# The modulation weights' tiles are loaded one step ahead of their multiplies, and the multiplies get a fixed place on VectorE

## The chip, the cores and the metric

The kernel runs on one core of a Trainium2 chip. The metric is the device time of one execution in microseconds (us); lower is better. Engines are named as in the profile: PE is TensorE's matmuls and PEld its weight loads, DVE is VectorE, ACT is ScalarE, POOL is GpSimd, and SP is SyncE, which here only issues DMA transfers (SPq is its queue).

## What is computed

Two transformer-like blocks run one after the other on 256 tokens of width 2048, in fp32. The part that matters here is the first block, whose normalised inputs, residuals and FFN are scaled by six vectors that come from a conditioning vector `c`:

```
silu_c = jax.nn.silu(c)                                    # [1, 2048]
mod_l = jnp.split(silu_c @ w_mod[l] + b_mod[l], 6, axis=-1) # w_mod: [2048, 6*2048]
hl  = modulate(rms_norm(xl, norm1_g[l]), mod_l[0], mod_l[1])
xl  = xl + mod_l[2][:, None, :] * mixer_output(...)
hl2 = modulate(rms_norm(xl, norm2_g[l]), mod_l[3], mod_l[4])
xl  = xl + mod_l[5][:, None, :] * sq_relu_ffn(hl2, w_ff1[l], b_ff1[l], w_ff2[l], b_ff2[l])
```

`mod_l[0]` and `mod_l[1]` are needed at once. The other four vectors, 64 tiles of 128 outputs, are needed only later: `mod_l[2]` to `mod_l[4]` in the output projection, `mod_l[5]` in the FFN.

## The kernel before

Every large matrix product goes through the same chunk of work. `weights` loads one chunk of a weight matrix, [128, 2048] fp32, as two halves of [128, 1024] (512 KB each) into the pool `raw`, which has four buffers, so two chunks. `split_w` makes two tiles out of each half: `wh`, a rounded copy that ScalarE writes (L198), and `wl`, what the rounding left out, which VectorE makes by a subtraction (L199). Both have three buffers. PE then multiplies by `wh` and by `wl`: in `gemm` (L213, L214) 16 pairs of matmuls per chunk with 512 and 256 columns, in `gemm_w` (L204 to L206) three of 258 columns. A `raw` buffer is free for its next load when its `wl` is done, so the load of a half waits for the subtraction of the half that stands four places ahead of it.

The 64 late tiles of the modulation don't go to PE. `w_mod` is stored with outputs on partitions, and for each tile VectorE multiplies two halves of [128, 1024] by a row `bc` that holds silu(c) on every partition, and sums along the row (`mod_tile`, a SCALAR_TENSOR_TENSOR with an accumulated output, L80 in the profile, since all VectorE calls go through a helper). Their tiles are called `mraw` and lie in the pool `aux`, which has two buffers. `qkv` puts 64 such steps into a list `fill`, and `weights` takes one of them out after every second chunk, 128 chunks in all: the query projection, the three branches of the mixer with their gates, the output projection and the first quarter of the FFN's first layer. In the trace that is the stretch from 353 us to 1233 us. A chunk with 512 + 256 columns and two of them between fillers are the unit below: "a step" is two chunks, four halves, one `w_mod` tile.

Nobody writes the order of the instructions by hand. A scheduler lays them out on each engine by priorities and dependencies; work inside `low()` has a low priority and goes where the scheduler finds room. `late` ties an instruction behind the last matmul that has been written so far, as an order for the scheduler alone, without a semaphore. Each engine then runs its instructions in that order, and SP issues all loads of `raw` and `mraw` in one queue.

Of the kernel before, what the change touches and what calls it, by code (L numbers as in the profile page):

```python
# [10 lines left out]
F32 = mybir.dt.float32  # L11
# [3 lines left out]
ALU = mybir.AluOpType  # L15
# [74 lines left out]
class Net:  # L90
# [65 lines left out]
            return self.vecs[:, o:o + c]  # L156
        return self.vecs[:, o + i:o + i + n]

    def late(self, inst):

        i = getattr(inst, "ins", inst)
        d = mybir.DependencyInfo(mybir.DependencyClass.NoSync, mybir.DependencyReason.SCHED_ONLY)
        self.tc.add_manual_dep(i, self.last_mm.name, d, reason="late")
        return inst

    def after(self, inst):

        i = getattr(inst, "ins", inst)
        d = mybir.DependencyInfo(mybir.DependencyClass.Sync, mybir.DependencyReason.DATA)
        self.tc.add_manual_dep(i, self.last_mm.name, d, reason="after")  # L170
        return inst
# [23 lines left out]
    def split_w(self, raw, n):  # L195
        h = self.wp.tile([P, 1024], F32R, name="wh", tag="wh", bufs=3)
        l = self.wp.tile([P, 1024], F32R, name="wl", tag="wl", bufs=3)
        self.nc.scalar.activation(h[:, :n], raw, AF.Copy)  # L198
        self.nc.vector.tensor_sub(l[:, :n], raw, h[:, :n].bitcast(F32))  # L199
        return h, l  # L200

    def mm3(self, ps, lh, ll, rh, rl, start, stop):
# [136 lines left out]
                                                            ap=[[0, P], [1, 2048]])))  # L339
        self.a.activation(self.bc, self.bc, AF.Silu)  # L340

    def mod_tile(self, i):

        for hf in range(2):
            s = slice(hf * 1024, hf * 1024 + 1024)
            raw = self.aux("mraw")
            self.late(self.nc.sync.dma_start(raw, self.ins["w_mod"][i][:, s]))
            self.v.scalar_tensor_tensor(raw, raw, 1.0, self.bc[:, s], op0=ALU.mult, op1=ALU.mult,
                                        accum_out=self.modt[:, i, hf:hf + 1])

    def startup(self):

# [137 lines left out]
    def qkv(self):  # L490
        v, a, ins = self.v, self.a, self.ins
        for m in range(2):
            pss = self.gemm(ins["w_k"][m], [self.hx, self.hc])
            for s, ps in enumerate(pss):
                a.activation(self.kT[1][:, 2 + m, s * T:s * T + T], ps, AF.Identity, bias=self.vec("b_in", 46 + m))
        self.vt = self.many("D2 A3", [P, 2, 1024], "vt")
        for g in range(2):
            vb = self.t2("vb")
            self.bcast_row(vb, "na_vb", g * 512)
            pss = self.gemm_tok([ins["w_v"][g, c] for c in range(4)], [self.hx, self.hc])  # L500
            s = slice(g * 512, g * 512 + 512)
            for i, ps in enumerate(pss):
                v.tensor_add(self.vt[i // 2][:, i % 2, s], ps, vb)
        self.q = self.at("C0", [P, 8, T], "q")
        self.load_bc()
        self.fill = [lambda i=i: self.mod_tile(i) for i in (*range(32, 80), *range(80, 96))]
        for m in range(8):
            ps, = self.gemm(ins["w_q"][m], [self.hx])
            v.tensor_scalar(self.q[:, m, :], ps, self.vec("b_in", 32 + m), 0.125, op0=ALU.add, op1=ALU.mult)
# [1038 lines left out]
```

## Time and profile before

| | |
|---|---|
| median of 3 runs | 2786.59 us (2778.81 to 2793.52) |
| profiled execution | 2797.3 us, span 2795.5 us |
| busy share of PE, DVE, ACT | 96%, 74%, 52% of the span |
| mean granted PE clock | 0.987 |
| largest wait of VectorE for a DMA | 168.8 us in 65 waits, for `mraw` |
| chain that ended last | PE 26%, DVE 2%, ACT 1% of the span; the rest of it is not shown there |

The three runs differ by 0.5% of their median. The profiled execution is 10.7 us above the median. A PE that counts as busy is one with a matmul under way by a modelled end, so gaps between matmuls are a lower bound of what PE loses.

### The profile page before, as it was taken

The page shows a single profiled execution, that of the slowest core. Times are in us where ns is not written, and L with a number is a line of the kernel's source. Part 1 is how long each engine was busy: PE and PEld are TensorE (multiplying, and loading weights), DVE is VectorE, ACT ScalarE, POOL GpSimd, SP SyncE. Part 2 cuts the span into 40 slices and gives each one's busy share as a digit, 9 for nine tenths or more (in the row PEclk, how much of TensorE's full clock was granted, in tenths as well). Part 3 has the DMA queues.
Part 4 walks back from the last instruction along what each step waited for, and adds up shares of the span by engine and source line. Part 5 has one row for each costly group of instructions (what it writes and reads, how often), then busy time and mean ns, then how long its engine had stood idle before and what let it go on. Part 6 is the DMA issues. An engine that isn't in the chain of part 4 may idle for free. (4 is left out here: it accounts for less than half of the span.)

```text
span 2795.5 us, 47178 instructions
## 1 busy us (share of the span) xinstructions
PE 2691.3 (96%) x18464; PEld 2340.2 (84%) x18464; DVE 2057.0 (74%) x3559; ACT 1440.0 (52%) x2242; POOL 116.1 (4%) x222
## 2 busy tenths in 40 slices
PE   7999999999998889999999999999999999999988
PEld 6888877777877777988989989988888888888876
DVE  4579886776866667766888777677656776767987
ACT  3243265566534445544544645665545554644754
POOL 0000001110000000000000000000000001110000
PEclk9999999999999999999999999999999999999999
DMA  9854377777767777777566676755455567775544
GB/s 378 318 158 132 123 240 230 247 244 264 249 245 246 242 245 252 249 240 212 183 197 211 211 218 213 224 175 164 155 181 167 173 199 232 239 232 193 161 137 146
DMA packets 161616, 595.66 MB, mean 213 GB/s; under 512 B 19441, under 2 KB 20481, under 8 KB 156657
## 3 DMA queue, kind: packets, MB, share of 16 engines
q1 hardware_dynamic: 145152, 539.03, 59.3%
q0 software_dynamic: 16096, 53.60, 5.6%
q8 instruction: 144, 2.36, 0.4%
q14 instruction: 80, 0.65, 0.1%
q10 hardware_dynamic: 144, 0.02, 0.0%
HBM read 571.60 MB, written 17.83 MB: 211 GB/s over the span
## 5 line engine op out<-in xcount | busy, mean ns | idle before, releaser
L198 ACT ACTIVATE wh<-raw 128x1024 fp32r<-128x1024 f32 x812 | 859.3, 1059 | 938.4 <-PE pg L213 513.7
L199 DVE TENSOR_TENSOR wl<-raw,wh 128x1024 fp32r<-128x1024 f32 x812 | 990.9, 1221 | 353.3 <-ACT wh L198 344.4
L213 PE MATMUL pg<-hx,wh 128*128 128x512 f32 x1312 | 477.3, 404 | 6.0 <-ACT kT L80 3.4
L214 PE MATMUL pg<-hx,wl 128*128 128x256 f32 x1312 | 376.6, 288 | 20.2 <-DVE wl L199 20.1
L213 PE MATMUL pg<-fa,wh 128*128 128x512 f32 x1024 | 358.3, 396 | 0.0
L213 PEld LDWEIGHTS pg<-hx,wh 128*128 128x128 f32 x1312 | 251.9, 193 | 65.5 <-ACT kT L80 3.6
L206 PE MATMUL pg<-fg,wl 128*128 128x258 f32 x1024 | 287.3, 281 | 7.2 <-DVE wl L199 7.2
L205 PE MATMUL pg<-fg,wh 128*128 128x258 f32 x1024 | 290.4, 284 | 0.0
L204 PE MATMUL pg<-fg,wh 128*128 128x258 f32 x1024 | 289.0, 283 | 0.0
L214 PE MATMUL pg<-fa,wl 128*128 128x256 f32 x1024 | 284.6, 279 | 1.2 <-DVE wl L199 1.2
L80 DVE SCALAR_TENSOR_TENSOR mraw<-mraw,bc 128x1024 f32<-128x1024 f32 x128 | 156.1, 1221 | 169.7 <-DMA mraw<-in_w_mod 168.8
L214 PEld LDWEIGHTS pg<-hx,wl 128*128 128x128 f32 x1312 | 253.2, 193 | 29.7 <-DVE wl L199 24.9
L213 PEld LDWEIGHTS pg<-fa,wh 128*128 128x128 f32 x1024 | 191.7, 188 | 45.3 <-issue 0.6
L213 PE MATMUL pg<-rg,wh 128*128 128x512 f32 x640 | 228.8, 399 | 0.2 <-ACT wh L198 0.2
L213 PE MATMUL pg<-ag,wh 128*128 128x512 f32 x640 | 228.2, 400 | 0.8 <-ACT wh L198 0.8
L206 PEld LDWEIGHTS pg<-fg,wl 128*128 128x128 f32 x1024 | 194.9, 191 | 8.5 <-DVE wl L199 8.4
L214 PEld LDWEIGHTS pg<-fa,wl 128*128 128x128 f32 x1024 | 192.8, 188 | 2.3 <-DVE wl L199 1.5
L205 PEld LDWEIGHTS pg<-fg,wh 128*128 128x128 f32 x1024 | 193.5, 189 | 0.1
L204 PEld LDWEIGHTS pg<-fg,wh 128*128 128x128 f32 x1024 | 192.5, 188 | 1.1 <-issue 1.0
L214 PE MATMUL pg<-rg,wl 128*128 128x256 f32 x640 | 181.3, 284 | 0.7 <-DVE wl L199 0.7
L214 PE MATMUL pg<-ag,wl 128*128 128x256 f32 x640 | 181.2, 283 | 0.0
L213 PEld LDWEIGHTS pg<-ag,wh 128*128 128x128 f32 x640 | 120.2, 188 | 29.5 <-ACT wh L198 1.1
(487 smaller groups left out, 4874.6 us busy)
## 6 DMA issues: line engine op xcount, KB each, us to landing
raw<-in_w_f SPq DMA_DIRECT2D x256, 512.0 KB, 4.6
mraw<-in_w_mod SPq DMA_DIRECT2D x128, 512.0 KB, 7.5
raw<-in_w_g SPq DMA_DIRECT2D x96, 512.0 KB, 6.2
raw<-in_w_mod SPq DMA_DIRECT2D x20, 1024.0 KB, 8.3
raw<-in_w_conv SPq DMA_DIRECT2D x32, 512.0 KB, 3.8
raw<-in_w_o SPq DMA_DIRECT2D x32, 512.0 KB, 6.2
raw<-in_w_gab SPq DMA_DIRECT2D x32, 512.0 KB, 3.8
raw<-in_w_abo SPq DMA_DIRECT2D x32, 512.0 KB, 4.4
```

The source lines that it names most:

```text
L80: r = f(*a, **kw)
L198: self.nc.scalar.activation(h[:, :n], raw, AF.Copy)
L199: self.nc.vector.tensor_sub(l[:, :n], raw, h[:, :n].bitcast(F32))
L204: mm(ps, lhsT=lh, rhs=rh, start=start, stop=False)
L205: mm(ps, lhsT=lh, rhs=rl, start=False, stop=False)
L206: i = mm(ps, lhsT=ll, rhs=rh, start=False, stop=stop)
L213: mm(ps, lhsT=lh, rhs=act.both(b), start=start, stop=False, skip_group_check=True)
L214: i = mm(ps[:, :T], lhsT=ll, rhs=act.hi(b), start=False, stop=stop, skip_group_check=True)
```

## The change

`mod_tile` is cut in two. `mod_load(i)` takes both `aux` buffers and issues the two loads of tile i. `mod_tile(i, then)` multiplies the halves that stand in the buffers, and after that calls `mod_load` for the next tile. The first load is issued ahead of the query projection. A second edit gives the multiplies a place: `split_w` remembers its last subtraction as `last_wl`, and each multiply is ordered behind it (`behind`, an order for the scheduler without a semaphore). The number of loads, multiplies and buffers stays.

```
-    def late(self, inst):
+    def behind(self, inst, other):
         i = getattr(inst, "ins", inst)
         d = mybir.DependencyInfo(mybir.DependencyClass.NoSync, mybir.DependencyReason.SCHED_ONLY)
-        self.tc.add_manual_dep(i, self.last_mm.name, d, reason="late")
+        self.tc.add_manual_dep(i, other.name, d, reason="behind")
         return inst
+    def late(self, inst):
+        return self.behind(inst, self.last_mm)
...
         self.nc.scalar.activation(h[:, :n], raw, AF.Copy)
-        self.nc.vector.tensor_sub(l[:, :n], raw, h[:, :n].bitcast(F32))
+        i = self.nc.vector.tensor_sub(l[:, :n], raw, h[:, :n].bitcast(F32))
+        self.last_wl = getattr(i, "ins", i)
...
-    def mod_tile(self, i):
-        for hf in range(2):
+    def mod_load(self, i):
+        self.mraw = [self.aux("mraw") for _ in range(2)]
+        for hf, raw in enumerate(self.mraw):
             s = slice(hf * 1024, hf * 1024 + 1024)
-            raw = self.aux("mraw")
             self.late(self.nc.sync.dma_start(raw, self.ins["w_mod"][i][:, s]))
-            self.v.scalar_tensor_tensor(raw, raw, 1.0, self.bc[:, s], op0=ALU.mult, op1=ALU.mult,
-                                        accum_out=self.modt[:, i, hf:hf + 1])
+    def mod_tile(self, i, then):
+        for hf, raw in enumerate(self.mraw):
+            s = slice(hf * 1024, hf * 1024 + 1024)
+            self.behind(self.v.scalar_tensor_tensor(raw, raw, 1.0, self.bc[:, s], op0=ALU.mult, op1=ALU.mult,
+                                                    accum_out=self.modt[:, i, hf:hf + 1]), self.last_wl)
+        if then is not None:
+            self.mod_load(then)
...
-        self.fill = [lambda i=i: self.mod_tile(i) for i in (*range(32, 80), *range(80, 96))]
+        self.mod_load(32)
+        self.fill = [lambda i=i: self.mod_tile(i, i + 1 if i < 95 else None) for i in range(32, 96)]
```

VectorE, before, near the end of the branch that `w_no` closes, the step whose wait stands at 860.30 us in the trace. The numbers are those of buffers: `wl_8232` and `wl_8238` are the halves of the newest chunk, `mraw_8241` and `mraw_8244` the tile of this step, and `raw_8297` and `raw_8303` the halves of the chunk after.

```order
L199 TENSOR_TENSOR wl_8232<-raw_8229,wh_8231 128x1024
L80 TENSOR_TENSOR pg_8141<-pg_8141,fold_8174 128x256
L199 TENSOR_TENSOR wl_8238<-raw_8235,wh_8237 128x1024
L80 SCALAR_TENSOR_TENSOR mraw_8241,modt_79<-mraw_8241,bc_3585 128x1024
L80 SCALAR_TENSOR_TENSOR mraw_8244,modt_79<-mraw_8244,bc_3585 128x1024
L199 TENSOR_TENSOR wl_8300<-raw_8297,wh_8299 128x1024
```

The same place now, on VectorE; `wl_8236` and `wl_8242` are the halves of the same chunk.

```order
L203 TENSOR_TENSOR wl_8236<-raw_8233,wh_8235 128x1024
L80 TENSOR_TENSOR pg_8145<-pg_8145,fold_8178 128x256
L203 TENSOR_TENSOR wl_8242<-raw_8239,wh_8241 128x1024
L80 SCALAR_TENSOR_TENSOR mraw_8141,modt_79<-mraw_8141,bc_3585 128x1024
L80 SCALAR_TENSOR_TENSOR mraw_8142,modt_79<-mraw_8142,bc_3585 128x1024
L203 TENSOR_TENSOR wl_8304<-raw_8301,wh_8303 128x1024
```

At this place nothing moved on VectorE: the pair stands behind the newest chunk's second half in both. Over the 64 steps, 63 pairs now stand together, 63 of them right behind a `wl`; before it was 21 pairs that stood together and 23 first multiplies right behind a `wl`, the others having short work between or ahead of them.

SP's queue of loads, before, around the loads of that tile; what a load waits for stands in brackets (DVE is a count that VectorE's instructions raise, DMAHW are counts of earlier DMAs).

```order
L185 DMA raw_8229<-in_w_no 128x1024 [waits DMAHW3_49,DMAHW1_49,DVE_49]
L185 DMA raw_8235<-in_w_no 128x1024 [waits DMAHW4_49,DMAHW2_49,DVE_49]
L185 DMA raw_8297<-in_w_g 128x1024 [waits DMAHW5_49,DVE_49]
L185 DMA raw_8303<-in_w_g 128x1024 [waits DMAHW6_49,DVE_49]
L347 DMA mraw_8241<-in_w_mod 128x1024
L347 DMA mraw_8244<-in_w_mod 128x1024
L185 DMA raw_8347<-in_w_g 128x1024 [waits DMAHW7_49,DMAHW1_49,DVE_49]
```

And the queue now, around the loads of the tile that is multiplied at the place shown.

```order
L189 DMA raw_8233<-in_w_no 128x1024 [waits DMAHW3_49,DVE_49]
L189 DMA raw_8239<-in_w_no 128x1024 [waits DMAHW4_49,DVE_49]
L352 DMA mraw_8141<-in_w_mod 128x1024 [waits DVE_49]
L352 DMA mraw_8142<-in_w_mod 128x1024 [waits DVE_49]
L189 DMA raw_8301<-in_w_g 128x1024 [waits DMAHW7_49,DMAHW5_49,DVE_49]
L189 DMA raw_8307<-in_w_g 128x1024 [waits DMAHW6_49,DMAHW0_49,DVE_49]
L189 DMA raw_8351<-in_w_g 128x1024 [waits DMAHW1_49,DVE_49]
```

Before, the loads of a step's tile stood behind those of the chunk that follows the step's newest one (8297, 8303) and waited for nothing of their own. Now they stand one chunk earlier, right behind the step's newest chunk (8233, 8239), and each waits for VectorE: for the multiply of the tile before, which holds its buffer.

## Rows read from the trace of the kernel before

**Rows 1.** The page: span, busy time, costly groups of `mraw` and `wl`

```profile
PE 2691.3 (96%) x18464; PEld 2340.2 (84%) x18464; DVE 2057.0 (74%) x3559; ACT 1440.0 (52%) x2242; POOL 116.1 (4%) x222
...
L199 DVE TENSOR_TENSOR wl<-raw,wh 128x1024 fp32r<-128x1024 f32 x812 | 990.9, 1221 | 353.3 <-ACT wh L198 344.4
...
L80 DVE SCALAR_TENSOR_TENSOR mraw<-mraw,bc 128x1024 f32<-128x1024 f32 x128 | 156.1, 1221 | 169.7 <-DMA mraw<-in_w_mod 168.8
```

**Rows 2.** Busy time by stretch: window, length, PE, PEld, DVE, ACT, POOL, clock, DMA share, GB/s

```profile
350.00:727.00 377.00, 368.34 (x1898) 291.58 (x1897) 275.75 (x489) 240.02 (x380) 35.57 (x66) 0.99 0.76 247
727.00:1120.00 393.00, 357.37 (x1941) 305.06 (x1941) 291.53 (x462) 183.05 (x292) 5.25 (x9) 0.97 0.72 244
1120.00:1233.00 113.00, 105.37 (x835) 102.44 (x833) 79.00 (x130) 61.60 (x94) 0.00 (x0) 1.00 0.74 250
1245.00:1500.00 255.00, 255.00 (x1701) 234.07 (x1700) 196.39 (x399) 120.89 (x153) 8.03 (x15) 1.00 0.63 199
1450.00:1500.00 50.00, 50.00 (x285) 43.44 (x284) 43.99 (x86) 18.76 (x18) 4.27 (x8) 1.00 0.65 209
2350.00:2400.00 50.00, 50.00 (x351) 43.93 (x350) 33.99 (x49) 25.75 (x33) 10.53 (x22) 1.00 0.83 282
```

**Rows 3.** VectorE around 860 us: start, duration, instruction, idle time and its releaser

```profile
846.49 1.23 DVE L80 SCALAR_TENSOR_TENSOR mraw<-mraw,bc 128x1024 f32<-128x1024 f32 x1 [3.24 <-DMA mraw<-in_w_mod]
...
854.31 1.22 DVE L199 TENSOR_TENSOR wl<-raw,wh 128x1024 fp32r<-128x1024 f32 x1
860.30 1.22 DVE L80 SCALAR_TENSOR_TENSOR mraw<-mraw,bc 128x1024 f32<-128x1024 f32 x1 [4.78 <-DMA mraw<-in_w_mod]
861.46 0.08 DVE L80 DVE_READ_ACCUMULATOR mraw<-mraw,bc 128x1 f32 x1
861.57 1.23 DVE L80 SCALAR_TENSOR_TENSOR mraw<-mraw,bc 128x1024 f32<-128x1024 f32 x1
862.72 0.08 DVE L80 DVE_READ_ACCUMULATOR mraw<-mraw,bc 128x1 f32 x1
862.72 1.22 DVE L199 TENSOR_TENSOR wl<-raw,wh 128x1024 fp32r<-128x1024 f32 x1
```

**Rows 4.** PE in the same stretch

```profile
850.39 0.39 PE L214 MATMUL pg<-hx,wl 128*128 128x256 f32 x1 [1.10 <-DVE wl L199]
...
863.99 0.39 PE L214 MATMUL pg<-hx,wl 128*128 128x256 f32 x1 [2.06 <-DVE wl L199]
```

**Rows 5.** SP's queue in the same stretch: first issue, length, merged issues

```profile
850.36 2.13 SPq L185 DMA_DIRECT2D raw<-in_w_g  x2
852.54 0.90 SPq L347 DMA_DIRECT2D mraw<-in_w_mod  x2
854.09 1.79 SPq L185 DMA_DIRECT2D raw<-in_w_g  x2
```

**Rows 6.** PE's waits, 727 to 1233 us: total, times, longest

```profile
PE pg L214 <- DVE wl L199: 34.6, 21, 3.4
PE pg L206 <- DVE wl L199: 7.2, 6, 1.7
PE pg L213 <- ACT wh L198: 0.8, 1, 0.8
```

**Rows 7.** PE's longest wait, 350 to 727 us

```profile
PE pg L214 <- DVE wl L199: 4.5, 4, 1.8
```

**Rows 8.** The subtraction of L199 by stretch: length, busy (count), clock, DMA share, GB/s

```profile
727.00:1233.00 506.00, 188.07 (x155) 0.97 0.73 246
1245.00:1500.00 255.00, 110.00 (x90) 1.00 0.63 199
```

**Rows 9.** Loads 727 to 1233 us: issues, KB each, median us to landing; then `mraw`'s spread

```profile
mraw<-in_w_mod SPq DMA_DIRECT2D x76, 512.0 KB, 7.6
raw<-in_w_g SPq DMA_DIRECT2D x56, 512.0 KB, 6.6
raw<-in_w_so SPq DMA_DIRECT2D x16, 512.0 KB, 8.1
...
DMA to landing us min/median/max: 5.3/7.6/11.0
```

**Rows 10.** The same, 1245 to 1500 us

```profile
raw<-in_w_f SPq DMA_DIRECT2D x90, 512.0 KB, 4.5
```

**Rows 11.** The tile `raw`, 727 to 1233 us: ScalarE's waits for a load

```profile
  DMA raw<-in_w_g: 7.6, 4
...
  DMA raw<-in_w_no: 2.3, 1
```

## Prediction

> **What bounds the kernel now.** I began with the page. PE is busy for 2691.3 of 2795.5 us [rows 1], so most of the kernel is limited by PE, and 104 us are left in which it visibly stands. The costly groups name a suspect: VectorE sat idle for 168.8 us ahead of the `mraw` multiplies until their DMA had landed [rows 1]. Idle time of VectorE counts only if PE waits for it, so I went to the windows by stretch. In the stretch of the 64 steps PE is short of full by 8.7 us from 350 to 727 us, by 35.6 us from 727 to 1120 us and by 7.6 us from 1120 to 1233 us; in the stretch right after it, where the same products run without `mraw`, PE is busy for 255.00 of 255.00 us [rows 2]. The waits say what ends PE's gaps: from 727 to 1233 us PE waited 34.6 + 7.2 us for a `wl`, in 27 waits, and 0.8 us for anything else [rows 6]; from 350 to 727 us, where attention shares PE, 4.5 us in 4 waits [rows 7].
>
> The timeline shows how the one becomes the other. SP issues the two `mraw` loads at 852.54 us [rows 5]. VectorE has nothing else to do ahead of the multiply from 855.5 us on, and the multiply starts at 860.30, after 4.78 us of waiting; its partner follows, and the next `wl` starts only at 862.72 [rows 3]. PE needs that `wl`, and stands for 2.06 us, to 863.99 [rows 4]. The step before has the same shape, smaller: 3.24 us of VectorE's wait become 1.10 us of PE's [rows 3, 4]. So about 2.1 to 2.7 us of such a wait are covered by the buffers of `wh` and `wl`, and what goes beyond comes out on PE. The reader should see that the pair itself, about 2.4 us from 860.30 to 862.72, is within what these buffers carry; it is the wait in front of it that isn't.
>
> **The change part by part.** *The load's lead.* Before, the tile's load stands behind the loads of the chunk after the step's newest one, so it is issued when the subtraction one chunk ahead has been done: a lead of about one chunk. At PE's pace a half takes 255 / 90 = 2.83 us [rows 8], so a chunk takes 5.7 us. A load of `mraw` lands 7.6 us after its issue in the median [rows 9]. 7.6 against 5.7 explains why VectorE waits in nearly every step. Now the load is issued as soon as the tile before has been multiplied, which is one step, four halves or 11.3 us, ahead of its own multiply, less the 1.2 us that the first multiply takes: 10.1 us. The second half is later by one multiply on both sides, so it has the same 10.1 us. Against 7.6 us in the median and 11.0 us at most [rows 9], the wait should be gone but for a few. I expect the landing to fall as well, since today two `raw` halves, two `mraw` halves and two more `raw` halves are issued within 5.5 us of each other, from 850.36 to 855.88 [rows 5], and then nothing for a while; with a VectorE that doesn't stall, the issues are spread over the step.
>
> By the Trainium skill, DMA: Bandwidth & Descriptors, Anatomy of one DMA, a transfer takes some 2.0 us and its bytes over 436 GB/s, so that an estimate for a lone half of 524,288 bytes is 3.2 us. By that price one chunk of lead would have been enough and there would be nothing to gain. The trace says 7.6, so the measurement decides, and the difference is queueing.
>
> *PE's waits.* What goes away at most is 34.6 + 7.2 + 4.5 = 46.3 us [rows 6, 7]. This is all of PE's waiting for a `wl`, though a few of these may not stem from `mraw`; from 1245 to 1500 us, without `mraw`, PE's busy time leaves none [rows 2].
>
> *The clock.* The granted clock is 0.97 from 727 to 1120 us and 0.99 from 350 to 727 us, and 1.00 from 1245 to 1500 us [rows 2]. Its two levels are 1.2 and 2.4 GHz, so 0.97 is a mean over short drops to the lower one. The drops stand in the stretches with waits; time lost is (1 - 0.97) x 393 + (1 - 0.99) x 377 = 11.8 + 3.8 = 15.6 us, within 4 us for the rounding of the shares. I count it as part of the gain. The Trainium skill, TensorE: Matmul & The Clock Gate, Part 1, says that the clock is held back by default and released by activity; by that rule the drops should leave with the gaps, and the trace agrees as far as it goes. Without the rule the sum would be 15.6 us smaller.
>
> *What the waits don't show.* As a check, 155 halves at 2.83 us are 439 us, and the stretch of 727 to 1233 us takes 506 [rows 8]: 67 us, where waits and clock there add up to 41.8 + 11.8 = 53.6. The other 13 us are small matmuls of the gated branch, which stay, and PE's start after each gap, which goes. Between nothing and 13 I take 4.
>
> *What stays or is new.* The multiplies, 128 of 1.22 us [rows 1], stay, and at the place shown in the order VectorE's sequence is the same. A pair that now always stands together holds a subtraction for up to 2.4 us; before, single multiplies with short work between held it for less, but they also waited. That costs nothing while the cover of 2.1 to 2.7 us holds, and if the short work that ScalarE needs (the sum of the two halves of a product, ahead of a gate's tanh) is stuck behind the pair, it costs some tenths of a us a step. New is the wait of SP: a load of `mraw` waits for the multiply of the tile before, and the `raw` loads queue behind it. The load that stands next needs the `wl` of the following chunk's first half, which VectorE makes after the multiplies anyway, so SP loses nothing by it. For late landings and a stuck sum together I take off a tenth of 62 us, 6 us; the ends for this are none and half, 31 us.
>
> The sum is 46.3 + 15.6 + 4 - 6 = 60 us. The profiled execution of 2797.3 us would become 2737; the median, which lies 10.7 us lower, 2786.6 - 60 = 2727 us, 2.1% less.
>
> **The rivals.** *VectorE takes the place of the wait.* From 727 to 1233 us VectorE is busy for 291.5 + 79.0 = 370.5 us [rows 2]. In 446 us that is 83%, and with an in-order engine a subtraction can be late at a lower share than 100%. For this speaks that the pair now comes in one piece. Against it, from 1450 to 1500 us VectorE is busy for 43.99 of 50 us, 88%, and PE is full [rows 2]; though that work is in shorter pieces. If half of the sum stays, the gain is 30 us: 2757 us. I give it 10%.
>
> *The bandwidth.* If a load takes 7.6 us because loads stand behind each other, issuing `mraw` earlier could just make the weights late. The Trainium skill, DMA: Bandwidth & Descriptors, Queues, rings and completion order, says that an engine consumes its descriptors in ring order, which would put a `raw` half behind both halves of `mraw`. In the rows, `raw` takes 6.6 us and up to 8.1 in the median with `mraw` around, 4.5 without [rows 9, 10], and ScalarE waited for a `raw` five times, 9.9 us in all [rows 11]. At the new pace the DMA share goes from 0.73 [rows 8] to 0.73 x 506 / 446 = 0.83, and one stretch of 50 us with just that share and 282 GB/s leaves PE full [rows 2]. If in every second of the 39 steps a half came late by 1.6 us, the spread of those medians between 8.1 and 6.5, it would cost 31 us: 2758 us. 6%.
>
> *The clock stays low*, since other small gaps remain: 44 us of gain, 2742 us. 8%; it lies within the range.
>
> *The other side.* The two buffers now make a loop: multiply, load into the same buffer, multiply. A step can't be shorter than the landing plus 1.2 us. At 7.6 us that is 8.8 and below PE's 11.3; it begins to show when the landing passes 10.1 us. Today a step takes 506 / 155 x 4 = 13.1 us [rows 8]; the loop would be slower than that from a landing of 11.9 us on, which is above the 11.0 at most of today [rows 9]. With 13.0 us in the middle the 39 steps from 727 to 1233 us would take 14.2 us each, 45 us more in all: about 2830 us. For it speaks that a late multiply makes the next load late, which before it didn't; against it every row on landings. 3%.
>
> *Nothing happens:* the scheduler puts work elsewhere in such a way that as much is lost, 2787 us. The three runs are 0.5% apart, so that 0.5%, 14 us, is about what can be told from no change. 4%.
>
> **How the numbers follow.** The forecast has 69%, the likeliest, and gives 2727 us. Faster by over 0.5% holds for it and the first three rivals, 93%, of which I take 2 off for a sum that is wrong in a way not listed: 0.91. Within 0.5% is 0.05, slower 0.04. The range's low end takes all of the 67 us, plus 4.5 us of waits and 3.8 us of clock from 350 to 727 us, 75 us, and some 6 us for the spread of runs: 2706. Its high end holds the rivals at 2757 and 2758 with the same spread: 2763. Outside of it lie the last two rivals and what is not listed.
>
> **What would show it right or wrong.** Right: VectorE's wait for `mraw` falls from 168.8 us to under 20 [rows 1]; PE's waits for a `wl` in the steps fall from 46 us to under 8; a step of the stretch after attention takes 11.2 to 11.5 us, not 13.1; the clock there is 1.00; `mraw` lands in 4.5 to 7 us. Wrong: VectorE's wait is gone but PE's isn't, with ScalarE or VectorE as releaser (first rival); ScalarE waits for `raw` by tens of us (second); `mraw` lands after over 10 us and VectorE's waits stay (other side). If the waits vanish and the stretch still takes over 470 us, I have taken for waiting what is PE's own work.

## The result and the profile after

The changed kernel takes 2721.7 us in the median of four runs (2720.79 to 2723.52); the kernel before takes 2788.3 us beside it. The ratio is 0.9767, with a 95% interval of 0.9751 to 0.9782: 2.3% faster. The profiled execution takes 2723.5 us, 73.8 us less than that of before. That one lay above its median, so the pair of profiles differs by more than the medians, which differ by 66.6 us.

The page, with the busy times and the `mraw` group that answer to [rows 1]; lines of the code have moved by some (L199 is L203 now, L213 and L214 are L218 and L219):

```profile
span 2721.5 us, 47183 instructions
PE 2669.0 (98%) x18464; PEld 2329.9 (86%) x18464; DVE 2060.2 (76%) x3559; ACT 1436.6 (53%) x2240; POOL 116.1 (4%) x222
...
L80 DVE SCALAR_TENSOR_TENSOR mraw<-mraw,bc 128x1024 f32<-128x1024 f32 x128 | 151.3, 1218 | 0.0
```

The multiplies are as many and as long as before, and the idle time ahead of them went from 169.7 us to 0.0. The view of the tile `mraw` has no line of VectorE waiting for a DMA any more, and loads land sooner (min, median, max; the median of before was 7.5 us over the same 128 loads):

```profile
L80 DVE SCALAR_TENSOR_TENSOR mraw<-mraw,bc x128: 1204/1219/1225, 360.4 to 1150.8; 128x1024 f32<-128x1024 f32 x128
...
DMA to landing us min/median/max: 4.4/6.0/7.9
```

The windows that answer to [rows 2], and the count of subtractions for [rows 8]. The steps end at 1152 us now, not at 1233, so the last windows are shorter:

```profile
350.00:727.00 377.00, 375.31 (x1967) 299.25 (x1966) 288.35 (x507) 245.34 (x387) 35.53 (x66) 1.00 0.77 254
727.00:1120.00 393.00, 392.42 (x2385) 348.77 (x2385) 332.75 (x529) 214.25 (x342) 5.25 (x9) 1.00 0.84 283
...
727.00:1160.00 433.00, 185.44 (x153) 1.00 0.83 280
```

PE is busy for 392.42 of 393 us where it was 357.37, and the clock is 1.00 in both stretches where it was 0.99 and 0.97. A half takes 433 / 153 = 2.83 us, the same as in the FFN without `mraw` [rows 8]; before it took 3.26. All of PE's waits from 350 to 1160 us:

```profile
PE pg L218 <- ACT wh L202: 0.8, 1, 0.8
PE pg L218 <- DVE vt L80: 0.5, 1, 0.5
PE pg L209 <- ACT wh L202: 0.4, 1, 0.4
PE sgp L649 <- DVE sv L80: 0.3, 1, 0.3
```

None is for a `wl`; before, those were 46.3 us [rows 6, 7]. The timelines of SP and of VectorE show the lead in one step:

```profile
843.01 1.47 SPq L352 DMA_DIRECT2D mraw<-in_w_mod  x2
845.29 2.52 SPq L189 DMA_DIRECT2D raw<-in_w_g  x2
```

```profile
851.89 1.22 DVE L203 TENSOR_TENSOR wl<-raw,wh 128x1024 fp32r<-128x1024 f32 x1 [1.24 <-ACT wh L202]
853.04 1.22 DVE L80 SCALAR_TENSOR_TENSOR mraw<-mraw,bc 128x1024 f32<-128x1024 f32 x1
854.18 0.08 DVE L80 DVE_READ_ACCUMULATOR mraw<-mraw,bc 128x1 f32 x1
854.18 1.22 DVE L80 SCALAR_TENSOR_TENSOR mraw<-mraw,bc 128x1024 f32<-128x1024 f32 x1
```

The load is issued at 843.01 us and multiplied from 853.04 us on: 10.0 us of lead, where the step at 860.30 us of before had 7.8 us from issue to start and had been waiting for 4.78 of these [rows 3, 5]. VectorE now waits ahead of the `wl` for ScalarE, which costs nothing, since PE is full.

### The profile page after: what moved, and what is told of

It is laid out like the page before. It is cut to its first block, busy times and chain, and to the rows that moved or that the text cites. A ratio compares the mean times of both kernels' runs of the same rounds, so it can differ in the third digit from the quotient of the medians.

```text
span 2721.5 us, 47183 instructions
## 1 busy us (share of the span) xinstructions
PE 2669.0 (98%) x18464; PEld 2329.9 (86%) x18464; DVE 2060.2 (76%) x3559; ACT 1436.6 (53%) x2240; POOL 116.1 (4%) x222
## 5 line engine op out<-in xcount | busy, mean ns | idle before, releaser
L203 DVE TENSOR_TENSOR wl<-raw,wh 128x1024 fp32r<-128x1024 f32 x812 | 991.4, 1222 | 415.6 <-ACT wh L202 407.2
L218 PE MATMUL pg<-hx,wh 128*128 128x512 f32 x1312 | 466.2, 397 | 4.3 <-ACT kT L80 2.9
L219 PE MATMUL pg<-hx,wl 128*128 128x256 f32 x1312 | 370.0, 283 | 0.1
L218 PE MATMUL pg<-fa,wh 128*128 128x512 f32 x1024 | 358.3, 396 | 0.0
L218 PEld LDWEIGHTS pg<-hx,wh 128*128 128x128 f32 x1312 | 246.4, 188 | 62.7 <-ACT kT L80 3.1
L219 PE MATMUL pg<-fa,wl 128*128 128x256 f32 x1024 | 284.5, 279 | 0.0
L219 PEld LDWEIGHTS pg<-hx,wl 128*128 128x128 f32 x1312 | 247.5, 189 | 4.4 <-issue 1.8
L218 PEld LDWEIGHTS pg<-fa,wh 128*128 128x128 f32 x1024 | 191.7, 188 | 45.4 <-issue 0.6
L218 PE MATMUL pg<-rg,wh 128*128 128x512 f32 x640 | 229.5, 400 | 0.2 <-ACT wh L202 0.2
L218 PE MATMUL pg<-ag,wh 128*128 128x512 f32 x640 | 228.3, 400 | 0.8 <-ACT wh L202 0.8
L219 PEld LDWEIGHTS pg<-fa,wl 128*128 128x128 f32 x1024 | 192.8, 188 | 0.8
L219 PE MATMUL pg<-rg,wl 128*128 128x256 f32 x640 | 181.9, 285 | 0.8 <-DVE wl L203 0.8
L219 PE MATMUL pg<-ag,wl 128*128 128x256 f32 x640 | 181.2, 283 | 0.0
L218 PEld LDWEIGHTS pg<-rg,wh 128*128 128x128 f32 x640 | 121.5, 190 | 28.2 <-ACT wh L202 0.6
```

Of the source, the lines that this page charges most:

```text
L203: i = self.nc.vector.tensor_sub(l[:, :n], raw, h[:, :n].bitcast(F32))
L218: mm(ps, lhsT=lh, rhs=act.both(b), start=start, stop=False, skip_group_check=True)
L219: i = mm(ps[:, :T], lhsT=ll, rhs=act.hi(b), start=False, stop=stop, skip_group_check=True)
```

## The experiments

The first theory was that the wait for the load is all that was lost, and that the lead of the load decides it. Its rivals: that the place of the multiplies on VectorE matters by itself, that the loads cost time by their traffic, and that VectorE just fits. Where a theory has a number below, it is that of the run's own expectation.

**The loads ahead, without the order behind the subtraction** (`e1_ahead_only`).

```
-            self.behind(self.v.scalar_tensor_tensor(raw, raw, 1.0, ...), self.last_wl)
+            self.v.scalar_tensor_tensor(raw, raw, 1.0, ...)
```

> The loads are issued by code one step ahead, but the multiplies are no longer ordered behind the newest subtraction. In the built program the scheduler then pulls each multiply forward by a whole step: the pair of a tile stands right behind the wl of the chunk before its load's neighbour, as in the kernel before, and the lead of a load is one chunk again, not two. Theory 1 (the lead decides, and it takes both edits to get it): VectorE waits 140 to 180 us for mraw, PE 35 to 50 us for wl, time 2775 to 2800 us, no change from before. Theory 2 (issuing the load earlier in the code is what helps, the order on VectorE is a detail): VectorE's wait under 40 us, time 2720 to 2740 us.

2782.2 us, ratio 0.999 (0.9977 to 1.0003): no change. VectorE and PE wait as they did before (the tile's waits, and PE's waits from 350 to 1240 us):

```profile
  DMA mraw<-in_w_mod: 155.9, 56
```

```profile
PE pg L219 <- DVE wl L203: 31.8, 30, 2.2
PE pg L211 <- DVE wl L203: 5.3, 6, 1.2
```

So issuing the load a step earlier in the code gives nothing by itself. The order in the built program shows why; first SP's queue, then VectorE at the place of the load's multiplies:

```
L189 DMA raw_8301<-in_w_g 128x1024 [waits DMAHW7_49,DVE_49]
L189 DMA raw_8307<-in_w_g 128x1024 [waits DMAHW0_49,DVE_49]
L352 DMA mraw_8247<-in_w_mod 128x1024
L352 DMA mraw_8248<-in_w_mod 128x1024
...
L203 TENSOR_TENSOR wl_8242<-raw_8239,wh_8241 128x1024
L80 SCALAR_TENSOR_TENSOR mraw_8247,modt_79<-mraw_8247,bc_3585 128x1024
L80 SCALAR_TENSOR_TENSOR mraw_8248,modt_79<-mraw_8248,bc_3585 128x1024
```

The load stands behind the chunk of `raw_8301` and `raw_8307`, and the multiply behind the `wl` of the chunk ahead of that one: one chunk of lead, the picture of before. The scheduler has moved the multiply a step forward along with its load.

**The order alone** (`e2_place_only`): the multiplies behind `last_wl`, each tile's load in the same step again.

```
     def mod_tile(self, i, then):
+        self.mod_load(i)
...
-        if then is not None:
-            self.mod_load(then)
...
-        self.mod_load(32)
```

> The multiplies are ordered behind the newest subtraction, and the loads are issued in the same step as their multiplies, as before. In the built program every engine's order is then that of the kernel before. Theory 1 (the lead decides): 2778 to 2795 us, VectorE waits 160 to 180 us for mraw. Theory 2 (the place of the multiplies on VectorE is a good part of the gain): under 2765 us.

2787.1 us, ratio 1.0002 (0.9988 to 1.0017). The built program has the order of before on every engine, row by row, so its trace is a second look at the kernel before (it is used below). Neither edit does anything alone; the gain comes from the two together, since the lead is what lies between a load's place on SP and its multiply's place on VectorE.

**The kernel before with a single load** (`e3_before_one_load`): the wait taken away at its root.

```
-            raw = self.aux("mraw")
-            self.late(self.nc.sync.dma_start(raw, self.ins["w_mod"][i][:, s]))
-            self.v.scalar_tensor_tensor(raw, raw, 1.0, ...)
+            self.v.scalar_tensor_tensor(self.mjunk, self.mraw, 1.0, ...)
...
+        self.mraw, self.mjunk = self.aux("mraw"), self.aux("mjunk")
+        self.late(self.nc.sync.dma_start(self.mraw, self.ins["w_mod"][32][:, :1024]))
```

> The kernel before, with the 128 loads of w_mod's late tiles left out: one half is loaded once, and all 128 multiplies read it and write to a spare tile, so mod_l[2] to mod_l[5] are wrong. No wait for a load, no order edge, 64 MB less traffic. Theory 1 (all that was lost was the wait for the load): 2715 to 2725 us, the same as the changed kernel within its noise, PE's waits for wl under 5 us, no drop of the clock in the stretch. Theory 2 (the traffic of the loads costs time too, which the changed kernel still pays): 2700 us or less. Theory 3 (the place behind the subtraction is needed): 2740 us or more.

2739.9 us, ratio 0.9831 (0.9815 to 0.9847), 15 us over the range of theory 1 and just at the edge of theory 3 (the place behind the subtraction is needed): no wait for a load is left, and the kernel is still 18 us slower than the changed one. The tile's view and the windows show why. The 128 multiplies, held by nothing, are over at 803 us, and from 680 to 740 us, where attention ends, PE is busy for 48 of 60 us at a clock of 0.86:

```profile
L80 DVE SCALAR_TENSOR_TENSOR mjunk<-mraw,bc x128: 1206/1219/1248, 358.6 to 801.8; 128x1024 f32<-128x1024 f32 x128
```

```profile
680.00:740.00 60.00, 47.91 (x222) 35.13 (x221) 53.50 (x104) 36.87 (x58) 4.82 (x9) 0.86 0.41 133
```

The waits there are those of attention's chain (PE's timeline): the transposes `pst` of the softmax wait for ScalarE's tile `bt`, and the product `po` with the values for VectorE's copy `pt`.

```profile
705.48 0.74 PE L555 MATMUL pst<-ident,bt 128*128 128x128 f32 x4 [1.97 <-ACT bt L80]
708.15 3.67 PE L568 MATMUL po<-pt,vt 128*64 128x256 f32 x8 [1.94 <-DVE pt L80]
718.32 1.11 PE L555 MATMUL pst<-ident,bt 128*128 128x128 f32 x4 [4.64 <-ACT bt L80]
721.81 3.68 PE L568 MATMUL po<-pt,vt 128*64 128x256 f32 x8 [2.38 <-DVE pt L80]
```

**The changed kernel with a single load** (`e6_after_one_load`): the same, with the order behind the subtraction kept.

```
+        if i > 32:
+            return
+        self.mraw, self.mjunk = [self.aux("mraw")] * 2, self.aux("mjunk")
...
-            self.behind(self.v.scalar_tensor_tensor(raw, raw, 1.0, ...), self.last_wl)
+            self.behind(self.v.scalar_tensor_tensor(self.mjunk, raw, 1.0, ...), self.last_wl)
```

> The changed kernel with its multiplies in their place behind the subtractions, but with the loads of the late w_mod tiles left out: one half is loaded once and all 128 multiplies read it (mod_l[2] to mod_l[5] are wrong). It differs from the kernel before with one load in the order on VectorE alone. Theory 1 (in that kernel the multiplies, held back by nothing, were pulled forward into attention and delayed its end, and neither traffic nor anything else of the loads costs time): 2716 to 2726 us, the last multiply starts after 1100 us, PE's waits for pst, po and bt under 3 us. Theory 2 (the kernel before loses time in attention for another reason, whatever the place of the multiplies): 2735 us or more. Theory 3 (the loads' traffic still costs the changed kernel time): 2710 us or less.

2722.2 us, ratio 0.9773 (0.9757 to 0.9788), the same as the changed kernel. The last multiply starts at 1151.7 us, and the window that was short in the run before is full:

```profile
L80 DVE SCALAR_TENSOR_TENSOR mjunk<-mraw,bc x128: 1207/1218/1228, 360.6 to 1151.7; 128x1024 f32<-128x1024 f32 x128
```

```profile
680.00:740.00 60.00, 60.00 (x327) 50.90 (x326) 55.83 (x84) 32.55 (x49) 3.61 (x6) 1.00 0.63 201
```

Between 727 and 1120 us its DMA share is 0.61, against 0.84 with all loads, and the kernel takes as long: the traffic costs nothing. And the order has a use of its own: it holds the multiplies back in attention once no load does. From 400 to 700 us VectorE spent 50.3 us on them here and 105.3 us in the run before, and attention's last `po` starts at 685 us here and at 725 us there:

```profile
L583 PE MATMUL po<-pt,vt x128: 378/380/432, 422.0 to 685.4; 128*64 128x256 f32 x128
```

```profile
L568 PE MATMUL po<-pt,vt x128: 379/379/690, 414.1 to 724.9; 128*64 128x256 f32 x128
```

One thing in the expectation does not hold: the two kernels differ in more than VectorE's order. SP's is the same, but the scheduler laid out ScalarE and PE anew as well, and in `e3_before_one_load` attention's last matmuls stand on PE from 704 to 725 us with no matmul of a chunk between them. So the 18 us are shown to be the edit's; how much of them is VectorE's time in the chain and how much PE's new order is not shown.

**A third multiply in each step** (`e4_three`).

```
+            for _ in range(2 - hf):
                 self.behind(self.v.scalar_tensor_tensor(raw, raw, 1.0, ...), self.last_wl)
```

> The changed kernel with three multiplies a step in place of two (the first half is multiplied twice, so the result is not the reference's): VectorE gets 64 x 1.22 = 78 us more work, and its busy share in the stretch after attention goes from some 84% to 95%. Theory 1 (about 2 to 2.7 us of delay on top of the pair are covered by the buffers of wh and wl, as the waits of before showed): 1.2 us more are hidden, 2720 to 2735 us, PE's waits for wl under 12 us. Theory 2 (VectorE is at its limit and the changed kernel only just fits): 2760 us or more, PE's waits for wl over 35 us.

2745.5 us, ratio 0.9855 (0.984 to 0.9869): 24 us slower than the changed kernel, more than the first theory allowed, but not by the second either, since PE waited for a `wl` only 1.6 us from 350 to 1240 us. The largest gaps stand at attention's end again (PE's waits from 680 to 760 us, and the window from 680 to 740 us with the clock at 0.94; the last `po` starts at 717.7 us, against 691.7 in the changed kernel):

```profile
PE pst L569 <- ACT bt L80: 1.9, 1, 1.9
PE po L582 <- DVE pt L80: 1.7, 1, 1.7
PE sgp L650 <- DVE sv L80: 1.6, 1, 1.6
PE pg L219 <- DVE wl L203: 0.8, 2, 0.5
```

```profile
680.00:740.00 60.00, 54.71 (x275) 43.25 (x274) 50.27 (x89) 36.44 (x57) 4.70 (x8) 0.94 0.68 230
```

**The third multiply after attention alone** (`e7_three_late`), the same loop with `range(2 if i >= 62 and hf == 0 else 1)`.

> The changed kernel with a third multiply a step, but only in the steps of tiles 62 to 95, which run after attention has ended (the first half of these is multiplied twice, so mod_l[3] to mod_l[5] are wrong in part): 34 x 1.22 = 41 us more on VectorE. Theory 1 (the run with three multiplies in every step lost its 24 us at attention's end, where VectorE's work is in a chain, and nothing in the steps after it): 2720 to 2728 us. Theory 2 (it lost them because VectorE is at its limit in all steps): 2732 us or more, with PE's waits for wl over 8 us.

2726.8 us, ratio 0.9789 (0.9773 to 0.9805): 41 us more of VectorE's work cost 5 us, and PE waited for a `wl` 0.4 us. By subtraction the other 19 us of the run before belong to the first 30 steps, which hold attention's end and last some 80 us beyond it, to 773 us.

**Four multiplies after attention** (`e8_four_late`), with `range(2 if i >= 62 else 1)`.

> The same with four multiplies in the steps of tiles 62 to 95 (both halves twice): 83 us more on VectorE. From the busy time of the changed kernel between 727 and 1120 us, 332.75 of 393 us, a step of 11.27 us holds 9.54 us of VectorE's work, and with two more multiplies 11.98 us, over PE's pace. Theory 1 (VectorE then limits a step by its sum): 0.7 us in each of 25 to 34 steps, 17 to 24 us, so 2738 to 2750 us, with VectorE over 97% busy there. Theory 2 (what counts is how long a subtraction is held, now 4.9 us, beyond the pair of 2.4 us and the 2.1 to 2.7 us covered): PE waits of some 0.5 us in most steps at a VectorE still below 97%, 2728 to 2740 us.

2740.5 us, ratio 0.9845 (0.982 to 0.987), 19 us over the changed kernel, or 0.55 us in each of 34 steps. VectorE is busy for 380.47 of 393 us, 97%:

```profile
727.00:1120.00 393.00, 382.61 (x2280) 335.56 (x2280) 380.47 (x628) 207.73 (x331) 5.24 (x9) 1.00 0.83 272
```

```profile
PE pg L219 <- DVE wl L203: 5.5, 7, 2.4
PE pg L211 <- DVE wl L203: 3.4, 2, 2.1
```

The time fits the sum of VectorE's work, and PE's waits are few and long, not small ones in most steps. That speaks for the first theory. But the busy share, 96.8%, is just under its mark of 97%, and the median lies only 0.5 us above the range of the second theory, while the four runs spread from 2736.6 to 2747.5 us. ScalarE also waited 24.3 us for loads of `raw` from 350 to 1240 us, where it was 3.8 us in the changed kernel. How far the sum, the held subtraction and these late loads limit this run stays open.

**One more transfer in each step** (`e5_more_load`), in `mod_load`; `dp` is a scratch pool in the device's memory, so this one is a copy within it:

```
+        more = self.dp.tile([P, 1024], F32, name="more", tag="more", bufs=2)
+        self.late(self.nc.sync.dma_start(more, self.ins["w_mod"][i][:, :1024]))
```

> The changed kernel with one more transfer a step: half a tile of w_mod, 512 KB, is copied within the device's memory to a scratch place that nothing reads, on the same queue. Transfers of a step go from 3 to 3.5 MB at 11.3 us, and the DMA share from 0.84 to 0.95 or so. Theory 1 (the bandwidth had room, as the second rival was put aside): mraw lands in under 8 us, ScalarE waits under 15 us more for raw, 2720 to 2735 us. Theory 2 (the changed kernel sits just below the limit of the transfers): raw lands over 8 us, ScalarE's waits for raw are over 40 us, 2745 us or more.

2725.2 us, ratio 0.9783 (0.9768 to 0.9799). The transfers have room: at a DMA share of 0.93 and 326 GB/s, PE is busy for 392.40 of 393 us and ScalarE waited for a `raw` once, 1.9 us. The room is not quite free: the run takes 3.5 us longer than the changed kernel, and the clock is 0.99 in this stretch.

```profile
727.00:1120.00 393.00, 392.40 (x2357) 347.86 (x2356) 329.55 (x523) 212.03 (x340) 5.25 (x9) 0.99 0.93 326
```

## Why the prediction was right

*The bound.* Right: PE's gaps in the steps were VectorE's waits for `mraw`, passed on. With the waits gone all of PE's waits for a `wl` are gone, and in the run in which VectorE's waits stayed (`e1_ahead_only`), PE's stayed with them.

*The lead.* 10.1 us were worked out, 10.0 us measured in the step shown and in the median of the steps from 727 us on. The landing was expected to fall to 4.5 to 7 us and fell to 6.0, 7.9 at most, so no load was late: over all 128 the tightest landed 1.3 us ahead of its multiply.

*The terms of the sum.* The sum was made against the profiled execution: 60 us, and it fell by 73.8. The waits of 46.3 us went as a whole, and the clock's 15.6 us too, since it is 1.00 in both stretches. The two small terms were mis-sized. Of the 13 us that neither waits nor clock explained I took 4; the stretch of before's 155 halves would now take 155 x 2.83 = 439 us in place of 506, so nearly all of them went, within some 3 us for the halves at the borders, and the small matmuls of the gated branch, which were to stay, take next to nothing. The 6 us taken off for late landings and a stuck sum were nothing. 46.3 + 15.6 + 13 is 75 us.

*Luck in the number.* Against the medians the forecast of 2727 us is 5 us off, and that is in part luck. The terms were read from an execution 10.7 us above the median, and the sum was taken from the median. The waits and the loss by the clock are not the same in every execution. `e2_place_only`, with the order of before, was profiled at 2781.6 us, and there PE waited for a `wl` 40.0 us in place of 46.3 (350 to 1233 us), at a mean clock of 0.990 in place of 0.987, by the rounded means some 8 us:

```profile
PE pg L219 <- DVE wl L203: 34.5, 28, 2.8
PE pg L211 <- DVE wl L203: 5.1, 5, 1.7
...
PE pg L210 <- DVE wl L203: 0.4, 1, 0.4
```

```profile
core 0: 2779.7 us, clock 0.990
```

So two misses worked against each other: the small terms were 15 us too low, and the large ones were too high for the median. With the full 75 us the forecast would have been 2712 us, 10 us under what was measured.

*What was put at nothing.* That SP waits for VectorE costs nothing holds: from 350 to 1160 us PE waited for a `wh` 1.2 us in all, and `raw` lands sooner than before (5.4 us in the median for `w_g`, 6.6 before). That a pair is covered by the buffers holds as well: three multiplies a step, after attention, cost 5 us in 34 steps.

*The change's second edit* I had read as a detail that leaves VectorE's order as it was at the place shown. That was too little. Without it the first edit gives nothing (`e1_ahead_only`), because it is what keeps a multiply from going along with its load; and with no loads in the way it is worth 18 us, lost at attention's end (`e3_before_one_load` against `e6_after_one_load`).

*The rivals.* VectorE as the next limit was weighed at a share of 83%; it is 85% now from 727 to 1120 us, and more work there cost 5 us at 92% and 19 us at 97% (the two runs with more multiplies after attention). The bandwidth was put aside rightly (`e5_more_load`, `e6_after_one_load`); the 6.5 us in its price is the median of `w_no`, which stands in none of the rows. The clock did not stay low. The loop through the two buffers would have needed a landing of over 10.1 us, and 7.9 was the most.

*The price of a lone half.* The 3.2 us by the Trainium skill, DMA: Bandwidth & Descriptors, Anatomy of one DMA, is given there for transfers that GpSimd issues; the loads here are SP's. In the quiet stretch from 1245 to 1500 us a half of `raw` took 3.5 us at least and 4.5 in the median [rows 10].

By the Trainium skill, TensorE: Matmul & The Clock Gate, Part 1, activity releases the clock. The runs agree in part: the mean was 0.97 before from 727 to 1120 us, 0.98 there in `e1_ahead_only` and 0.86 at attention's end in `e3_before_one_load`, all with gaps on PE, and it is 1.00 where PE is full, in the changed kernel and in `e6_after_one_load` at attention's end. But not all gaps cost clock: it was 1.00 with PE busy for 105.37 of 113 us before [rows 2] and for 382.61 of 393 us in `e8_four_late`. So that the drops left with the gaps is seen; which gap brings a drop is not shown.

## What to carry to other kernels

Filler work on an engine that feeds the bound is free only as long as it and its waits stay within what the buffers between the two engines cover, here some 2.1 to 2.7 us beyond the filler itself, by two steps of the kernel before; a wait for a DMA uses that up first. The lead of a load is the distance between two places, that of the load on its queue and that of its user on its engine; when a scheduler sets both, moving the load in the code may move the user with it, so look at the built order of both and tie the user down. And when a wait is taken away, see what it had held back: here it had held the filler back in a stretch where another chain, attention's, then ended later.

## What the runs showed that was not expected

The prediction did not have that the place of the multiplies matters once no load holds them back (18 us at attention's end). That loads would land sooner was forecast; new is that they do so at a higher rate: from 727 us to the end of the steps `mraw` landed in 7.6 us at 246 GB/s before [rows 8, 9], and in 5.9 us at 280 GB/s after. Two issues on SP's queue stand up to 9.7 us apart there before and up to 5.4 us after; that the even spread is the cause is not shown. Also, 326 GB/s over 393 us, a share of 0.93, cost no more than 3.5 us.
